# Hymba layer: later-half queries alone in the recurrence levels, and another order of heads and projection steps

## The chip, the cores and the metric

The kernel runs on one core of a Trainium2 chip. The core has five engines with a queue of their own: TensorE (PE in the profile, with its weight loads as PEld), VectorE (DVE), ScalarE (ACT), GpSimd (POOL) and SyncE (SP), which here only issues DMAs. They wait for each other through semaphores. The metric is the device time of one execution in microseconds, the median of several runs.

## The reference

One decoder layer on 1024 tokens, behind 16 meta tokens (T = 1040 positions), with width 1024: a half-step feed-forward, one input projection, two groups of heads in parallel, an output projection, and a second half-step feed-forward. Of the two groups, four HGRN2 recurrence heads (key and value width 128) concern us, and the output projection that follows. In one head, with f the forget gate, k, q, v from the projection, and blocks of 128 tokens:

```python
bcum = jnp.cumsum(lf, axis=-2)                    # lf = log f, inside a block
o_inter = jnp.einsum('bhtd,bhdv->bhtv', qk * jnp.exp(bcum), S)
decay = jnp.exp(jnp.where(causal, diff, -jnp.inf))        # diff = bcum_t - bcum_s
attn = jnp.einsum('bhtd,bhsd,bhtsd->bhts', qk, kk, decay)
o_intra = jnp.einsum('bhts,bhsv->bhtv', attn, vk)
S_new = (jnp.exp(b_last[:, :, 0, :])[..., None] * S
         + jnp.einsum('bhsd,bhsv->bhdv', kk * jnp.exp(b_last - bcum), vk))
```

The output o = o_inter + o_intra is normed per head, multiplied by a gate, and joined with the other group's output; then h = h + o @ W_out. Everything is float32.

## The kernel before, in words

The kernel goes through its stages one after the other: first feed-forward, input projection beside the other group's heads, the recurrence heads beside half of the output projection, the rest of that projection, second feed-forward. The change lies in the fourth of these stages, and only there does the order of instructions differ.

**One recurrence head** (`hgrn_attend`, from L799) keeps keys `KB`, queries `QA`, gates `F` and values `vT` in SBUF, with the key dimension on the partitions and time along the free dimension. Loads L805 go through SP's queue; buffers have three copies, so head 3 uses those that head 0 leaves. The steps, each ended by a `yield` with an estimated time of work and a delay in ns:

1. loads; 2. the values are turned by PE (`flip`, L1036) and copied to `vr`.
3. The diagonal of `attn`: products of keys and queries for the 8 blocks of 128 tokens, masked with the identity (L833). Then POOL multiplies the queries with their gates (L839).
4. Seven levels n = 1, 2, ..., 64 (`LEVELS`). In level n a block is cut into pieces of 2n tokens. Queries in the later half of a piece see keys in its earlier half; the decay between them is already in `QA` and `KB`. The products of level n (L827) are taken for all pairs of a block, and a mask picks those of the level (L836, a copy under a byte mask). Afterwards POOL multiplies the later-half queries (L854) and DVE the earlier-half keys (L858) with the products of gates over their half, and DVE halves the table of gate products `Ts` (L864).
5. The keys are turned (`km` L870, `knp` L877), the gate values are loaded into the buffer of `KB` (L880).
6. The states `S`, in the buffer of `F`: PE makes the updates (`up` L891), DVE adds them in a chain of seven (L894).
7. and 8. The outputs, four blocks at a time (L904, L907); ACT squares them (L912), ACT and DVE make the norm.
9. and 10. The outputs are turned back (L923), multiplied with the gate (L925) and split into a rounded part and a rest (L930 on ACT, L931 on POOL).

In step 4, before, four blocks share a PSUM tile of 128 x 512, so a level takes two tiles and two masked copies. The pool `pz2` has two such banks; turns and states share two banks of `ptr2`, outputs two of `po2`.

**The order.** PE's order is written out by `weave`: it is the order in which the steps are called. `weave` keeps a clock of estimated work, a list of heads with the time at which each is due, and a filling stream: the steps of the output projection with the other group's half of o (`mix_out`, k0 = 4, 64 steps of three products each, 16 additions L1210 with a residual from DRAM). Heads 0, 1 and 2 are three lanes; head 3 follows head 0 in its lane. If no head is due, the filling stream goes on, as long as its share of its total is not over the heads' share of theirs (`work`); otherwise the head that is due first takes a step. The orders on the other engines are found by the framework's scheduler from the same program.

Of the kernel before, what the change touches and what calls it, by code (L numbers as in the profile page):

```python
# [39 lines left out]
class Block:  # L40
# [756 lines left out]
    def hgrn_attend(self, h, pool, src, oH):  # L797
        nc = self.nc

        def tile_of(name, n):  # L800
            return pool.tile([P, n], F32, tag=name, name=name, bufs=3)
# [2 lines left out]
        for t, x in ((vT, "v"), (KB, "k"), (QA, "q"), (F, "f")):  # L804
            nc.sync.dma_start(t, src[x][h])  # L805
        vr = tile_of("vr", SEQ).rearrange("p (c d) -> p c d", d=P)
        attn = [tile_of(f"attn{i}", 512).rearrange("p (c t) -> p c t", t=P) for i in range(2)]
        Ts = tile_of("Ts", T // 2 + T // 4 + T // 8 + T // 16 + SEQ // 32 + SEQ // 64 + 16)
        vm, kms = (
            pool.tile([META, P], F32, tag=x, name=x, bufs=3) for x in ("vm", "kms")  # L810
# [8 lines left out]
            nc.scalar.copy(vr[:, 4 * q : 4 * q + 4, :], ps)  # L819
        yield 960, 500  # L820

        def level(i):
            for half in range(2):
                ps = self.pz.tile([P, 4, P], F32, tag="z", name="lvl")
                for j in range(4):
                    c = 4 * half + j
                    nc.tensor.matmul(  # L827
                        ps[:, j, :], KB[:, META + c * P : META + (c + 1) * P],
                        QA[:, c * P : (c + 1) * P], start=True, stop=True,
                    )  # L830
                if i is None:
                    m = self.ident.unsqueeze(1).broadcast_to([P, 4, P])
                    nc.vector.tensor_mul(attn[half], ps, m)  # L833
                else:
                    m = self.masks[:, i, :].unsqueeze(1).broadcast_to([P, 4, P])
                    nc.vector.copy_predicated(attn[half], m, ps)  # L836

        level(None)
        nc.gpsimd.tensor_mul(QA, QA, F[:, META:])  # L839
        yield 1740, 3200  # L840
        tn = F
        at = 0
        for i, n in enumerate(LEVELS):
            level(i)
            if n <= 8:
                kb = KB.rearrange("p (b h r) -> p b h r", h=2, r=n)
                tk = tn[:, : T // n].rearrange("p (b h) -> p b h", h=2)
            else:
                kb = KB[:, META:].rearrange("p (b h r) -> p b h r", h=2, r=n)
                tk = tn[:, 1 : 1 + SEQ // n].rearrange("p (b h) -> p b h", h=2)  # L850
            nb = kb.shape[1]
            qa = QA.rearrange("p (b h r) -> p b h r", h=2, r=n)
            nq = qa.shape[1]
            nc.gpsimd.tensor_mul(  # L854
                qa[:, :, 1, :], qa[:, :, 1, :],
                tk[:, nb - nq :, 0:1].broadcast_to([P, nq, n]),
            )
            nc.vector.tensor_mul(  # L858
                kb[:, :, 0, :], kb[:, :, 0, :], tk[:, :, 1:2].broadcast_to([P, nb, n])
            )  # L860
            o = 0 if n <= 8 else 1
            nt = Ts[:, at : at + nb + o]
            at += nb + o
            nc.vector.tensor_mul(nt[:, o : o + nb], tk[:, :, 0], tk[:, :, 1])  # L864
            tn = nt
            yield 1740, 2600
# [390 lines left out]
    def weave(self, fill, streams=(), total=0.0, work=0.0):  # L1257

        clock = spent = done = 0.0
        live = [[0.0, s] for s in streams]
        ended = []
        join = None
        filling = True
        while live or filling:
            live.sort(key=lambda e: e[0])  # L1270
            if join is not None and any(e is join for e in ended):
                join = None
            ready = bool(live) and live[0][0] <= clock
            even = not work or spent * work <= (done + 6000) * total
            if not ready and filling and join is None and (even or not live):
                step = next(fill, None)
                if step is None:
                    filling = False
                elif isinstance(step, tuple):
                    if step[0] == "start":  # L1280
                        live.append([clock, step[1]])
                    elif not any(e is step[1] for e in ended):
                        join = step[1]
                else:
                    clock += step
                    spent += step
                continue
            entry = live[0]
            clock = max(clock, entry[0])
            step = next(entry[1], None)  # L1290
            if step is None:
                live.remove(entry)
                ended.append(entry[1])
            else:
                clock += step[0]
                done += step[0]
                entry[0] = clock + step[1]

    def run(self):
# [20 lines left out]
        with ExitStack() as c0:  # L1320
# [217 lines left out]
            with tc.manual_schedule(engines={nc.tensor.engine}), ExitStack() as cx:  # L1538
                with ExitStack() as c1:
                    mix = self.pool("mix2", ctx=c1)  # L1540
                    self.weights("wo", 2, 2, c1)
                    ho = self.pool("ho", ctx=c1)
                    oH.extend([ho.tile([P, 4, 512], F32R, name=f"oH{x}{i}") for i in range(2)]
                              for x in range(2))
                    self.pproj = self.pool("pproj2", 2, PSUM, c1)

                    def from_dram(half):
                        got = []
                        for i in range(2):
                            t = self.pool_o.tile([P, 4, 512], F32R, name=f"oT{half}{i}")  # L1550
                            nc.sync.dma_start(
                                t.bitcast(F32),
                                oD[:, :, i, 512 * half : 512 * half + 512]
                                .rearrange("k p t -> p k t"),
                            )
                            got.append(t)
                        return got

                    def first_half_of_o():
                        o = [from_dram(half) for half in range(2)]  # L1560
                        yield 5000.0
                        plan = [(m, half) for m in range(KT) for half in range(2)]
                        for t, f in self.mix_out(4, plan, o, {}, hD, hT, mix):
                            f()
                            yield t

                    with ExitStack() as c2:
                        c2.push(hg_ctx)
                        self.pool_o = self.pool("oT", ctx=c2, side="right")
                        self.pz = self.pool("pz2", 2, PSUM, c2)  # L1570
                        self.ptr = self.pool("ptr2", 2, PSUM, c2)
                        self.po = self.pool("po2", 2, PSUM, c2)
                        lanes = [chain(heads[0], heads[3]), heads[1], heads[2]]
                        self.weave(first_half_of_o(), lanes, 64 * 650.0 + 5000.0, 4 * 20000.0)
                    xa = self.pool("xs_a", ctx=cx, side="right")
                    operands(xa, ("B11", "B21"))
                    ev0 = self.pool("ev0", ctx=cx, side="right")
                    pre = ExitStack()
                    px = self.pool("pre", ctx=pre, side="right")
                    pps = self.pool("pps", 2, PSUM, c1)  # L1580
                    sums = [px.tile([P, n], F32, tag="nacc", name="nacc", bufs=2) for _ in "ab"]

                    def summed(half, c):

                        plan = [(m, half) for m in range(KT)]
                        steps = self.mix_out(0, plan, oH, ws, hD, hT, mix)
                        for i, (_, f) in enumerate(steps):
                            f()
                            if i % 4 == 3 and i > 3:
                                self.square(sums[half], hT, i // 4 - 1, c, n, px)  # L1590
                            yield i
                        self.square(sums[half], hT, KT - 1, c, n, px)

                    ws = {}
                    self.weights("wo2", 2, KT, c1)
                    drain(summed(0, cA))
                    blocks = iter(())
                    for i in summed(1, cB):
                        if i == 4:
                            r = self.inv_rms_rows(sums[0], n, px, pps)  # L1600
                        if i == 7:
                            r = self.spread_rows(r, n, px, pps)
                            blocks = self.blocks_a(hT, self.g2, cA, n, r, ops)
                        if i % 2:
                            next(blocks, None)
                    drain(blocks)
# [67 lines left out]
```

## Time and profile before

| | us |
|---|---|
| median of 3 runs | 2162.69 (2160.17 to 2167.77) |
| the profiled execution, its own time | 2161.26 |
| its span, first to last instruction | 2159.5 |
| from the first diagonal product of heads 0 to 2 to the end of their last level | 1273.86 to 1335.69 |
| from there to head 3's diagonal | 1335.69 to 1377.18 |
| head 3's diagonal and levels beside the output projection | 1377.18 to 1414.40 |
| rest of head 3, to the end of that half of the projection | 1414.40 to 1440 |

Times inside the trace are us from the start of the span. A row of a timeline has the start, the duration of the merged group, the engine, the line, the operation, its tiles and the number of merged instructions; in brackets stands the idle time before it and what ended it. A float32 product appears as two records on PE. The granted TensorE clock was 0.991 of full speed over the execution.

### The profile page before, as it was taken

To read this page: it belongs to the slowest core of one execution; us is meant where nothing else is said; L and a number is where in the kernel's file an instruction comes from. 1 tells how busy PE (TensorE), PEld (TensorE's weight loads), DVE (VectorE), ACT (ScalarE), POOL (GpSimd) and SP (SyncE) were. 2 spreads that over 40 slices of the span, in tenths; PEclk is the share of its full clock that TensorE was granted. 3 is DMA by queue.
4 is the path that set the end of the run, shared out by engine and by line. 5 is a ranking of instruction groups with operands and counts; after the bars stand their busy time and mean duration, and the time that the engine had idled before them with its cause. 6 is when DMAs were issued, how large, how long until landed. Compare 5 with 4: busy or idle time off the path is not lost.

```text
span 2159.5 us, 32075 instructions
## 1 busy us (share of the span) xinstructions
PE 2053.0 (95%) x11520; PEld 1838.6 (85%) x11520; DVE 1384.6 (64%) x2058; ACT 892.5 (41%) x1809; POOL 701.7 (32%) x764
## 2 busy tenths in 40 slices
PE   6899999999999999999999987899899999999998
PEld 6899999999999989987787876777678888878887
DVE  5775554554589842256766668658867667677674
ACT  8543333333465534455656520324323323334443
POOL 2265545452000313233332333312455445440000
PEclk9999999999999999999999999999999999999999
DMA  6543333334867636433443161233533333248363
GB/s 173 164 153 116 123 104 102 100 120 147 258 207 219 211 102 187 148 109 97 130 130 112 50 250 40 88 108 114 179 103 107 99 107 113 89 166 297 102 202 135
DMA packets 263440, 300.19 MB, mean 139 GB/s; under 512 B 24657, under 2 KB 189521, under 8 KB 262769
## 3 DMA queue, kind: packets, MB, share of 16 engines
q1 hardware_dynamic: 244784, 244.88, 37.0%
q0 software_dynamic: 17456, 53.26, 6.8%
q8 instruction: 91, 1.49, 0.3%
q14 instruction: 69, 0.56, 0.1%
q10 hardware_dynamic: 1040, 0.00, 0.0%
HBM read 215.96 MB, written 82.11 MB: 138 GB/s over the span
## 4 chain that ended last, share of the span: by engine, by line
PE 41%; DVE 6%; issue 2%; ACT 2%; POOL 1%; DMA 1%; SPq 0%; DVEq 0%; POOLq 0%; ACTq 0%
PE o L586 9%; PE qb L319 8%; PE qc L319 5%; PE qa L319 5%; PE lvl L827 2%; PE wo L163 1%; PE wo L164 1%; PE wo L162 1%; PE proj L162 1%; DVE keep L1179 1%; PE proj L163 1%; PE proj L164 1%; PE flip L1036 1%; DMA vT<-hg_v 1%; POOL sig L1182 1%
## 5 line engine op out<-in xcount | busy, mean ns | idle before, releaser
L319 PE MATMUL qb<-T,wh 128*128 128x344 f32 (+1 forms) x1056 | 312.7, 359 | 14.2 <-DVE u L361 10.3
L278 DVE TENSOR_TENSOR wl<-s,wh 128x512 fp32r<-128x512 f32 x176 | 202.9, 1153 | 117.7 <-ACT wh L276 114.9
L319 PEld LDWEIGHTS qb<-T,wh 128*128 128x128 f32 x1056 | 193.7, 190 | 40.5 <-ACT wh L276 8.9
L586 PE MATMUL o<-th,wh 128*128 128x344 f32 (+1 forms) x616 | 218.5, 356 | 4.0 <-DVE hT L596 4.0
L586 PE MATMUL o<-tl,wh 128*128 128x344 f32 (+1 forms) x616 | 218.5, 356 | 3.4 <-DVE tl L517 3.4
L586 PE MATMUL o<-th,wl 128*128 128x344 f32 (+1 forms) x616 | 218.3, 356 | 0.9 <-DVE wl L517 0.7
L319 PE MATMUL qa<-B,wh 128*128 128x344 f32 (+1 forms) x704 | 210.2, 363 | 0.0
L162 PE MATMUL proj<-xh,wh 128*128 128x344 f32 (+2 forms) x576 | 204.9, 356 | 0.9 <-ACT xh L1412 0.9
L276 ACT CAST wh<-s 128x512 fp32r<-128x512 f32 x176 | 109.4, 621 | 226.4 <-PE qb L319 157.3
L164 PE MATMUL proj<-xl,wh 128*128 128x344 f32 (+2 forms) x576 | 199.5, 346 | 0.4 <-POOL xl L1413 0.4
L163 PE MATMUL proj<-xh,wl 128*128 128x344 f32 (+2 forms) x576 | 199.8, 347 | 0.0
L278 DVE TENSOR_TENSOR wl<-raw,wh 128x512 fp32r<-128x512 f32 x172 | 152.2, 888 | 71.8 <-ACT wh L276 67.9
L319 PE MATMUL qb<-T,wl 128*128 128x344 f32 (+1 forms) x528 | 188.7, 357 | 0.0
L276 ACT CAST wh<-raw 128x512 fp32r<-128x512 f32 x172 | 106.0, 620 | 198.4 <-PE qc L319 97.8
L319 PE MATMUL qd<-X,wh 128*128 128x352 f32 x704 | 181.8, 326 | 0.0
L515 ACT CAST th<-act 128x512 fp32r<-128x512 f32 (+2 forms) x176 | 95.1, 542 | 181.0 <-PE o L586 128.2
L291 POOL TENSOR_TENSOR s<-raw 128x512 f32<-128x512 f32 x88 | 120.4, 1368 | 106.5 <-DVE wl L278 73.2
L517 DVE TENSOR_TENSOR tl<-act,th 128x512 fp32r<-128x512 f32 (+2 forms) x176 | 109.9, 628 | 65.6 <-ACT th L515 65.5
L319 PEld LDWEIGHTS qa<-B,wh 128*128 128x128 f32 x704 | 129.5, 190 | 16.0
L1182 POOL TENSOR_TENSOR sig<-sig,keep 128x144 f32<-128x144 f32 (+3 forms) x64 | 80.2, 1253 | 177.9 <-DVE keep L1179 114.0
L586 PEld LDWEIGHTS o<-tl,wh 128*128 128x128 f32 x616 | 116.3, 189 | 17.3 <-DVE tl L517 5.3
L319 PE MATMUL qa<-B,wl 128*128 128x344 f32 (+1 forms) x352 | 127.0, 361 | 4.0 <-DVE wl L278 4.0
(328 smaller groups left out, 4971.4 us busy)
## 6 DMA issues: line engine op xcount, KB each, us to landing
raw<-in_ffn_w_in_dram SPq DMA_DIRECT2D x208, 256.0 KB, 3.0
raw<-in_ffn_w_out_dram SPq DMA_DIRECT2D x176, 256.0 KB, 4.0
raw<-in_w_in_dram SPq DMA_DIRECT2D x28, 512.0 KB, 3.8
ks<-kD SPq DMA_DIRECT2D x32, 260.0 KB, 5.3
ak<-in_ffn_w_out_dram SPq DMA_DIRECT2D x22, 256.0 KB, 4.9
hT<-xD SPq DMA_DIRECT2D x8, 520.0 KB, 9.3
xD<-xts POOLq DMA_DIRECT2D x16, 256.0 KB, 3.0
vD<-vhl SPq DMA_DIRECT2D x8, 512.0 KB, 4.7
```

Source lines behind the costliest of these rows:

```text
L162: nc.tensor.matmul(ps, wh[:, s], xs, start=k == 0, stop=False)
L163: nc.tensor.matmul(ps, wl[:, s], xs, start=False, stop=False)
L164: nc.tensor.matmul(ps, wh[:, s], xl[:, k, c0 : c0 + n], start=False, stop=k == nk - 1)
L276: nc.scalar.copy(hi, src)
L278: nc.vector.tensor_sub(lo, src, hi.bitcast(F32))
L291: op(t, x, y)
L319: nc.tensor.matmul(ps, a[:, k, :], b[:, k0 + k, :], start=start and k == 0 and i == 0, stop=k == 3 and i == 2, skip_group_check=True,)
L515: nc.scalar.copy(hi, src)
L517: nc.vector.tensor_sub(lo, src, hi.bitcast(F32))
L586: nc.tensor.matmul(banks[bank][m], y[:, m * P : (m + 1) * P], z, start=start and q == 0 and e == 0, stop=q == nq - 1 and e == 2, skip_grou ...
L827: nc.tensor.matmul(ps[:, j, :], KB[:, META + c * P : META + (c + 1) * P], QA[:, c * P : (c + 1) * P], start=True, stop=True,)
L1182: nc.gpsimd.tensor_mul(sig, sig, keep[:, 1 : nk + 1])
```

## The change

Four things change.

- The diagonal keeps its two tiles, in a function of its own. A level computes products for later-half queries alone: 64 of the 128 columns of a block, so all 8 blocks fit one tile of 128 x 512 (one bank). One masked copy then goes over all eight blocks, and touches only the later-half columns of `attn`. For that the two `attn` tiles of a head become one of 1024 columns.
- `weave`, where it has a budget (`work`), takes among the heads that are due the one in the lowest lane, where it took the one that was due first.
- The budget for the four heads goes from 4 x 20000 to 4 x 21900.
- What follows from these for the order on PE: heads 0 and 1 start their diagonal before head 2 turns its values, and head 2 runs about a level behind them. Two steps of the projection come behind the key turns of heads 0 and 1, two behind the last level of head 2, one before and one after the second output halves of heads 0 and 1, four behind their last turns. Where the two orders differ they have the same 16 steps. From head 3's second level on the order is the same as before.

```diff
@@ -804,7 +804,8 @@
         vr = tile_of("vr", SEQ).rearrange("p (c d) -> p c d", d=P)
-        attn = [tile_of(f"attn{i}", 512).rearrange("p (c t) -> p c t", t=P) for i in range(2)]
+        at8 = tile_of("attn", SEQ).rearrange("p (c t) -> p c t", t=P)
+        attn = [at8[:, 4 * i : 4 * i + 4, :] for i in range(2)]
@@ -819,7 +820,7 @@
-        def level(i):
+        def diagonal():
             for half in range(2):
                 ps = self.pz.tile([P, 4, P], F32, tag="z", name="lvl")
                 for j in range(4):
@@ -828,20 +829,33 @@
                         ps[:, j, :], KB[:, META + c * P : META + (c + 1) * P],
                         QA[:, c * P : (c + 1) * P], start=True, stop=True,
                     )
-                if i is None:
-                    m = self.ident.unsqueeze(1).broadcast_to([P, 4, P])
-                    nc.vector.tensor_mul(attn[half], ps, m)
-                else:
-                    m = self.masks[:, i, :].unsqueeze(1).broadcast_to([P, 4, P])
-                    nc.vector.copy_predicated(attn[half], m, ps)
-
-        level(None)
+                m = self.ident.unsqueeze(1).broadcast_to([P, 4, P])
+                nc.vector.tensor_mul(attn[half], ps, m)
+
+        def later(x, n):
+
+            return x.rearrange("p (b h r) -> p b h r", h=2, r=n)[:, :, 1, :]
+
+        def level(i, n):
+            ps = self.pz.tile([P, 8, P // 2], F32, tag="z", name="lvl")
+            for c in range(8):
+                nc.tensor.matmul(
+                    ps[:, c, :].rearrange("p (b r) -> p b r", r=n),
+                    KB[:, META + c * P : META + (c + 1) * P],
+                    later(QA[:, c * P : (c + 1) * P], n), start=True, stop=True,
+                )
+            nb = P // (2 * n)
+            m = later(self.masks[:, i, :], n).unsqueeze(1).broadcast_to([P, 8, nb, n])
+            out = at8.rearrange("p c (b h r) -> p c b h r", h=2, r=n)[:, :, :, 1, :]
+            nc.vector.copy_predicated(out, m, ps.rearrange("p c (b r) -> p c b r", r=n))
+
+        diagonal()
         nc.gpsimd.tensor_mul(QA, QA, F[:, META:])
         yield 1740, 3200
...
         for i, n in enumerate(LEVELS):
-            level(i)
+            level(i, n)
@@ -1261,13 +1275,17 @@
         clock = spent = done = 0.0
-        live = [[0.0, s] for s in streams]
+        live = [[0.0, s, i] for i, s in enumerate(streams)]
...
         while live or filling:
-            live.sort(key=lambda e: e[0])
+            if work:
+                live.sort(key=lambda e: (max(e[0] - clock, 0.0), e[2]))
+            else:
+                live.sort(key=lambda e: e[0])
@@ -1278,7 +1296,7 @@
                     if step[0] == "start":
-                        live.append([clock, step[1]])
+                        live.append([clock, step[1], 0])
@@ -1571,7 +1589,7 @@
                         lanes = [chain(heads[0], heads[3]), heads[1], heads[2]]
-                        self.weave(first_half_of_o(), lanes, 64 * 650.0 + 5000.0, 4 * 20000.0)
+                        self.weave(first_half_of_o(), lanes, 64 * 650.0 + 5000.0, 4 * 21900.0)
```

## The prediction

> **What bounds the kernel now.** I read the page first, then the busy time by stretch around the changed stage, then the tile of the level products, then that stage engine by engine in order of time.
>
> ```profile
> span 2159.5 us, 32075 instructions
> PE 2053.0 (95%) x11520; PEld 1838.6 (85%) x11520; DVE 1384.6 (64%) x2058; ACT 892.5 (41%) x1809; POOL 701.7 (32%) x764
> ```
>
> On average PE is the bound with 95%, so a change that relieves DVE would be worth nothing. The average hides the stage that is changed:
>
> ```profile
> core 0: us, PE busy (x) PEld busy (x) DVE busy (x) ACT busy (x) POOL busy (x), PEclk, DMA share, GB/s
> 1269.14:1273.86 4.72, 3.87 (x28) 2.84 (x27) 3.44 (x11) 3.03 (x6) 0.00 (x0) 1.00 1.02 390
> 1273.86:1335.69 61.83, 50.76 (x386) 46.37 (x385) 58.82 (x76) 2.08 (x4) 31.11 (x23) 0.97 0.30 103
> 1335.69:1377.18 41.49, 31.41 (x227) 26.68 (x225) 23.41 (x52) 19.57 (x69) 8.06 (x7) 1.00 0.30 97
> 1377.18:1414.40 37.22, 37.22 (x228) 32.82 (x227) 28.80 (x40) 2.57 (x5) 11.84 (x9) 1.00 0.30 86
> 1414.40:1440.00 25.60, 25.03 (x139) 20.69 (x137) 11.69 (x24) 7.97 (x26) 1.42 (x2) 1.00 0.32 93
> ```
>
> Each row has the length of a stretch, then the busy time of PE, PEld, DVE, ACT and POOL. From 1273.86 to 1335.69 heads 0 to 2 go through the diagonal and the seven levels: DVE is busy 58.82 of 61.83 us, PE 50.76. Here DVE is the bound. From 1335.69 to 1377.18 the heads build their states and outputs, and PE is idle 10.1 of 41.49 us. From 1377.18 on head 3 runs alone between steps of the output projection, and PE is full: nothing can be gained there except by less PE work. So at most 11.1 + 10.1 + about 1.4 us = 23 us of PE idle time lie in reach, 1% of the span.
>
> ```profile
> L827 PEld LDWEIGHTS lvl<-QA,KB x512: 186/192/338, 1273.8 to 1411.4; 128*128 128x128 f32 x171
> L827 PE MATMUL lvl<-QA,KB x512: 270/275/553, 1273.9 to 1411.5; 128*128 128x128 f32 x171
> L836 DVE COPY_PREDICATED attn<-masks,lvl x56: 710/722/746, 1283.9 to 1411.8; 128x512 f32<-128x512 uint8 x56
> L833 DVE TENSOR_TENSOR attn<-lvl,ident x8: 673/688/692, 1275.0 to 1379.9; 128x512 f32<-128x512 f32 x8
> ```
>
> 256 products appear as 512 records, two to an fp32 product; 56 masked copies are 4 heads x 7 levels x 2 halves. One beat late in the three-head stretch, DVE, then POOL, then PE:
>
> ```profile
> 1315.57 0.74 DVE L836 COPY_PREDICATED attn<-masks,lvl 128x512 f32<-128x512 uint8 x1 [0.16 <-PE lvl L827]
> 1316.19 1.13 DVE L858 TENSOR_TENSOR KB<-KB,Ts 128x520 f32<-128x520 f32 x1
> 1317.25 1.32 DVE L836 COPY_PREDICATED attn<-masks,lvl 128x512 f32<-128x512 uint8 x2
> 1318.47 0.88 DVE L858 TENSOR_TENSOR KB<-KB,Ts 128x512 f32<-128x512 f32 x1
> 1319.27 0.73 DVE L836 COPY_PREDICATED attn<-masks,lvl 128x512 f32<-128x512 uint8 x1
> ```
>
> ```profile
> 1315.67 1.10 POOL L854 TENSOR_TENSOR QA<-QA,Ts 128x512 f32<-128x512 f32 x1 [1.61 <-issue]
> 1317.72 1.08 POOL L854 TENSOR_TENSOR QA<-QA,Ts 128x512 f32<-128x512 f32 x1 [0.95 <-PE lvl L827]
> ```
>
> ```profile
> 1313.51 4.07 PE L827 MATMUL lvl<-QA,KB 128*128 128x128 f32 x32 [0.70 <-DVE attn L836]
> 1318.10 4.07 PE L827 MATMUL lvl<-QA,KB 128*128 128x128 f32 x32 [0.53 <-DVE attn L836]
> ```
>
> PE does two heads (32 records) in 1318.10 - 1313.51 = 4.59 us, 2.29 us a head-level, and each time waits for a masked copy to free one of two PSUM banks. Copies that follow each other start 0.61 us apart (1317.25 + 1.32 - 0.72 = 1317.85). The KB update takes longest when POOL works: both KB rows end 0.55 us after a POOL product ends (1316.77 to 1317.32; 1318.80 to 1319.35).
>
> **The change part by part.**
>
> *Masked copies.* A level has one copy over 512 elements in place of two: 28 fewer on DVE, 21 of them in the three-head stretch, where DVE is the bound. Each frees a slot of 0.61 us: 21 x 0.61 = 12.8 us. The new copy writes 512 elements in runs of n with steps of 2n, and reads the mask so. No row shows a stepped masked copy; the nearest are the KB updates, which at n = 1 work on every second element:
>
> ```profile
> L858 DVE TENSOR_TENSOR KB<-KB,Ts x17: 680/1070/1427, 1294.0 to 1334.5; 128x520 f32<-128x520 f32 x9, 128x512 f32<-128x512 f32 x8
> L858 DVE TENSOR_TENSOR KB<-KB,F x3: 680/1519/1549, 1285.4 to 1292.0; 128x520 f32<-128x520 f32 x3
> L854 POOL TENSOR_TENSOR QA<-QA,Ts x18: 1048/1088/1300, 1293.5 to 1336.0; 128x512 f32<-128x512 f32 x18
> L854 POOL TENSOR_TENSOR QA<-QA,F x3: 1498/1508/1512, 1284.9 to 1289.9; 128x512 f32<-128x512 f32 x3
> ```
>
> Their least time is 680 ns for the stepped 520 (the F row, n = 1) as for the later ones with long runs, so a step costs DVE nothing there. POOL does mind: 1508 at n = 1 against 1048 at n = 64. I take 0.72 for the new copy. The ends are 0.72 and, if it slowed as POOL does, 0.72 x 1508/1048 = 1.04, which takes 21 x 0.32 = 6.7 us back if all levels had it; most have longer runs, so about 3.
>
> *Level products.* 224 products go from 128 moving columns to 64; each still loads the same 128 columns of KB. Whether that saves PE time is told by products with fewer moving columns:
>
> ```profile
> 1489.45 1.05 PE L175 MATMUL nps<-ones_d,nacc 128*128 128x1 f32 x8 [2.23 <-DVE nacc L210]
> 1405.29 1.95 PE L827 MATMUL lvl<-QA,KB 128*128 128x128 f32 x16
> 1409.85 1.95 PE L827 MATMUL lvl<-QA,KB 128*128 128x128 f32 x16
> ```
>
> With one moving column eight records take (1.05 - 0.25)/7 = 0.114 us each; with 128 moving columns sixteen take (1.95 - 0.27)/15 = 0.112 (0.25 and 0.27 for the last record's own time; its PEld stream is as long). One column costs as much as 128: loading the weights sets the pace. So 64 columns cost 0.112 too, and I book 0. The ends: 0, and half the stream, 16 x 0.056 = 0.9 us a head-level. The moving operand is also read in steps; at twice the time a column it would still lie under the load.
>
> The Trainium skill, "TensorE: Matmul & The Clock Gate", section "LDWEIGHTS (loading the stationary operand)", puts a load at columns/1.2 ns, 107 ns for 128, whatever moves; the trace agrees (112). The table under "Back-to-back issue gap" of the same page lets a matmul fall with its moving columns, to about 60 cycles for 64 or fewer; taken alone it speaks for a gain on PE, which the one-column rows contradict.
>
> *Three-head stretch, sum.* DVE: 61.83 - 12.8 = 49.0 us. The floor is PE: 3 heads x 8 x 16 records x 0.112 = 43.0 us. So DVE still sets it, with little over; -12.8 stands, and -18.8 is its end.
>
> *One bank a level.* Two levels instead of one are in flight in two banks, so the bank wait is for the copy of the head before last. Booked at nothing of its own: DVE's queue behind it sets the time.
>
> *The order of heads.* Heads 0 and 1 now start their diagonal before head 2 turns its values, and head 2 stays a level behind. On POOL its gate product moves behind two level-1 products:
>
> ```profile
> 1275.89 7.44 POOL L839 TENSOR_TENSOR QA<-QA,F 128x1024 f32<-128x1024 f32 x3 [21.28 <-PE lvl L827]
> ```
>
> 2.5 us each, so head 2 waits 2 x 1.5 = 3.0 us longer; PE has the second level of heads 0 and 1 in front (2 x 1.8 us), so it costs 0; uncovered it costs 3.0. On DVE head 2's small Ts products now stand between level copies, and what waits behind them is the next copy and its bank; there are as many as before, so 0.
>
> *States and outputs.* PE's order from here until head 3's second level has the same products and the same 16 output-projection steps; only their places differ. Before, the output products wait for squares:
>
> ```profile
> 1358.80 0.46 PE L904 MATMUL op<-F,QA 128*128 128x128 f32 x2 [2.51 <-ACT sq L912]
> 1363.84 0.46 PE L904 MATMUL op<-F,QA 128*128 128x128 f32 x2 [1.23 <-ACT sq L912]
> 1350.69 2.71 DVE L894 SCALAR_TENSOR_TENSOR F<-F,Ts,up 128x128 f32<-128x128 f32 x7 [0.61 <-PE up L891]
> ```
>
> Now head 2's turns and a projection step stand between the two halves of heads 0 and 1, so 2.51 + 1.23 = 3.7 us go. What is late next: the transposes of head 0's output come right behind head 2's state products and need their two banks, which DVE's chain of seven (2.71 us) frees; PE stands there about 2.7 us. Net -1.0, ends -6 and +5.
>
> *DMAs.* SP's queue gets a weight load and a residual load among the gate loads, and head 3's four loads stay behind all three gate loads:
>
> ```profile
> L805 SPq DMA_DIRECT2D F<-hg_f x4: 319/350/461, 1256.9 to 1363.2; - x4
> DMA to landing us min/median/max: 3.2/7.8/10.4
> ```
>
> Head 3's F goes into head 0's buffer, free after head 0's second output half. DVE's next use of it, the first Ts product of head 3, stands ahead of head 2's state updates and head 0's gain. By my walk it is reached some 5 us after the issue, so the 3.2 to 5 us that a lone pair needs is covered, the 10.4 of twelve loads together is not: 0, ends 0 and +5.
>
> *The tail.* From head 3's second level on the order is the same, four projection steps between levels, and PE stays full (levels start 1409.85 - 1405.29 = 4.56 us apart). 0. The budget's new constant moves only steps ahead of it.
>
> **Sum.** -12.8 + 0 - 1.0 + 0 = -13.8 us on the profiled execution: 2159.5 + 1.8 around it = 2161.3, so 2147.5. The median of the three runs, 2162.7, lies 1.4 above that execution; I say 2148.
>
> **Rivals.**
>
> *PE gains too.* If 64 columns take half the stream, each of head 3's seven levels shrinks by 0.9: 6.3 us in the full stretch, and about 1 where DVE sets the time: 2140. Against it stand the one-column rows.
>
> *POOL takes the gain back.* With one copy, KB starts 0.61 after the copy. If DVE has once fallen behind by a little, KB of one head meets POOL's product for the next, starts after it, and ends 0.55 behind its end; then copy, bank, products follow in a ring of two banks: 0.61 + 1.7 (copy late) + 0.14 + 1.94 = 4.4 us for two head-levels, 2.2 each in place of 2.29. Then 15 head-levels gain 0.09 and the first six 0.61: 1.4 + 3.7 + 1.0 = 6 us, 2155. The rows with KB 0.55 behind POOL speak for it; against it, that PE's pace of 1.8 leaves 0.2 us a head-level, enough to stay in step.
> The Trainium skill, "SBUF — State Buffer", section "Who interferes with whom", says that a DVE instruction with two SBUF inputs and a GpSimd instruction that reads SBUF block each other wholly, the first to issue winning; the KB rows agree for POOL first, and no row shows POOL held by KB.
>
> *Slower: the steps.* A masked copy with steps of 2n and byte masks is in no row. At three times its time, 2.2 us, it loses 2.2 - 1.33 = 0.87 against the two old ones: 21 x 0.87 = 18 us, 2178. It decides from 1.33 us a copy (no gain), and from 1.69 the kernel is measurably slower. The KB rows speak against it.
>
> *The queue stands.* Head 3's F late by 5 us: 2153.
>
> **How the numbers follow.** Forecast 0.50 (2143 to 2153 alone); PE gains 0.13; POOL 0.20, on the line between faster and same; queue 0.07; steps 0.10. A difference under 0.3% (6.5 us) can't be told from none here. Faster: 0.50 + 0.13 + 0.07 + half of 0.20 = 0.80; same 0.11 (the other half and a tenth of the steps); slower 0.09. The range 2137 to 2160 leaves out the steps and the outer halves of the others.
>
> **What would show it.** Right: L836's successor has 28 copies near 0.72; the 64-column records stay 0.11 apart; the three-head stretch is near 49 us with PE above 85% busy; head 3's levels stay 4.56 apart. Wrong: copies above 1 us, KB updates mostly above 1.3 us with head-levels 2.2 apart, a DVE wait of microseconds on head 3's F, or 64-column records at 0.06.

## The result, and the profile after

The changed kernel takes 2181.07 us (median; 2179.71 to 2182.60) beside 2163.99 us for the kernel before: ratio 1.0079, 95% interval 1.0059 to 1.0099. It is slower by 0.8%, where 2148 us and a gain of 0.7% were forecast. The profiled execution of it has a span of 2178.0 us, 18.5 more than before.

The head of the page of the changed kernel, and its row of granted clocks in 40 slices:

```profile
span 2178.0 us, 32021 instructions
...
PE 2078.3 (95%) x11520; PEld 1867.5 (86%) x11520; DVE 1365.1 (63%) x2030; ACT 892.1 (41%) x1809; POOL 701.6 (32%) x764
...
PEclk9999999999999999999999985999999999999999
```

DVE has 28 instructions and 19.5 us of work less, as the change means it to. PE has the same 11520 records and 25.3 us more of busy time. The row of clocks points at the reason: two slices, 54 us each, stand at 8 and 5 tenths; the execution's mean clock is 0.976, before 0.991.

Busy time by stretch for the changed kernel: the three heads from their first diagonal product to the first key turn, then on to head 3's key turn; below it 20 us inside the three heads, and the same 20 us of the kernel before.

```profile
core 0: us, PE busy (x) PEld busy (x) DVE busy (x) ACT busy (x) POOL busy (x), PEclk, DMA share, GB/s
1272.68:1350.66 77.98, 72.69 (x379) 72.24 (x378) 47.82 (x57) 3.15 (x6) 30.15 (x22) 0.60 0.24 87
1350.66:1433.14 82.48, 72.98 (x470) 63.54 (x470) 48.06 (x89) 22.14 (x73) 20.69 (x16) 0.95 0.29 90
...
1300.00:1320.00 20.00, 20.00 (x96) 20.00 (x95) 11.27 (x12) 0.00 (x0) 7.11 (x6) 0.50 0.00 1
```

```profile
1300.00:1320.00 20.00, 16.17 (x127) 14.59 (x125) 19.71 (x26) 0.00 (x0) 8.70 (x8) 1.00 0.06 14
...
1335.69:1414.42 78.73, 68.65 (x455) 59.50 (x452) 52.21 (x92) 22.14 (x73) 19.89 (x15) 1.00 0.30 91
```

The three-head stretch takes 77.98 us in place of 61.83: +16.2. The next one takes 82.48 in place of 78.73: +3.8; its first 8.7 us still run at half clock. The first product starts 1.2 us earlier (1272.68 after 1273.86), and what follows head 3's key turn is 0.2 shorter: together the 18.5 us. In the 20 us the bound has changed hands. Before, DVE was busy 19.71 of 20 us and PE did 127 records at a clock of 1.00. Now PE is busy without a break, does 96 records at 0.50, and DVE is idle 8.7 us.

PE of the changed kernel in order of time, from head 2's turns into the levels:

```profile
1280.24 0.66 PE L1050 MATMUL flip<-ident,vT 128*128 128x128 f32 x4 [3.05 <-DVE vm L817]
1280.73 6.86 PE L842 MATMUL lvl<-QA,KB 128*128 128x64 f32 x32
1287.39 3.72 PE L828 MATMUL lvl<-QA,KB 128*128 128x128 f32 x16
1290.91 3.75 PE L842 MATMUL lvl<-QA,KB 128*128 128x64 f32 x32
1296.90 49.48 PE L842 MATMUL lvl<-QA,KB 128*128 128x64 f32 x235 [2.24 <-DVE attn L850]
```

The last row holds 235 records without a pause: (49.48 - 0.42)/234 = 0.210 us each on average (the first microsecond still at full clock), where 0.112 was forecast; a head-level of 16 takes 3.4 us in place of the 2.29 of before. The 32 records at 1290.91 have 64 columns too and took (3.75 - 0.27)/31 = 0.112. So it isn't the width as such: the same product costs 0.112 or 0.210, by the clock. The trace's clock record has 0.5 from 1280.8 for 10.2 us and from 1297.9 for 61.4 us, 0.6 and 1.0 us after the end of a pause of PE (3.05 and 2.24 us). The first of these stretches outlasts 6.9 us of 64-column products and ends, at 1291.0, within head 2's diagonal, whose products have 128 columns. The second pause ended with a masked copy, for which DVE came late: ahead of it stood a product of head 2's table `Ts` and a split of projection weights.

```profile
1291.76 2.09 DVE L878 TENSOR_TENSOR Ts<-Ts 128x260 f32<-128x260 f32 x1
1293.77 1.78 DVE L149 TENSOR_TENSOR wl<-raw,wh 128x512 fp32r<-128x512 f32 x1
1295.47 1.28 DVE L850 COPY_PREDICATED attn<-masks,lvl 128x512 f32<-128x512 uint8 x1
```

Later in the levels DVE waits for PE each time, and the copies are shorter:

```profile
1327.01 0.70 DVE L850 COPY_PREDICATED attn<-masks,lvl 128x512 f32<-128x512 uint8 x1 [1.68 <-PE lvl L842]
1327.62 1.13 DVE L872 TENSOR_TENSOR KB<-KB,Ts 128x512 f32<-128x512 f32 x1
1330.43 0.71 DVE L850 COPY_PREDICATED attn<-masks,lvl 128x512 f32<-128x512 uint8 x1 [1.68 <-PE lvl L842]
```

Head 3's levels, which alternate with four projection steps, stay at full clock and 4.57 us apart:

```profile
1405.70 1.90 PE L842 MATMUL lvl<-QA,KB 128*128 128x64 f32 x16
...
1410.28 1.89 PE L842 MATMUL lvl<-QA,KB 128*128 128x64 f32 x16
...
1414.85 1.89 PE L842 MATMUL lvl<-QA,KB 128*128 128x64 f32 x16
```

A pause and a lowered clock stand in the trace of before as well, at the same place. Its PE row, and its busy times in the 3.4 us at which its clock record has 0.5:

```profile
1281.87 5.60 PE L827 MATMUL lvl<-QA,KB 128*128 128x128 f32 x32 [2.17 <-DVE attn L833]
```

```profile
1282.80:1286.20 3.40, 3.40 (x17) 3.18 (x17) 3.25 (x6) 0.00 (x0) 1.81 (x2) 0.50 1.05 386
```

There it came back after 3.4 us, over products of 128 columns. That difference is what the experiments are about.

### The profile page after: what moved, and what is told of

Same layout as the page of the kernel before. It is cut to its first block, busy times and chain, and to the rows that moved or that the text cites. A ratio compares the mean times of both kernels' runs of the same rounds, so it can differ in the third digit from the quotient of the medians.

```text
span 2178.0 us, 32021 instructions
## 1 busy us (share of the span) xinstructions
PE 2078.3 (95%) x11520; PEld 1867.5 (86%) x11520; DVE 1365.1 (63%) x2030; ACT 892.1 (41%) x1809; POOL 701.6 (32%) x764
## 4 chain that ended last, share of the span: by engine, by line
PE 44%; DVE 5%; issue 2%; ACT 1%; POOL 1%; DMA 0%; SPq 0%; DVEq 0%; POOLq 0%; ACTq 0%
PE o L586 9%; PE qb L319 8%; PE qa L319 5%; PE qc L319 5%; PE lvl L842 3%; PE proj L162 1%; PE proj L163 1%; PE proj L164 1%; PE wo L162 1%; PE wo L163 1%; PE wo L164 1%; DVE keep L1193 1%; PE flip L1050 1%; PE oacc L1124 1%; POOL sig L1196 1%
## 5 line engine op out<-in xcount | busy, mean ns | idle before, releaser
L319 PE MATMUL qb<-T,wh 128*128 128x344 f32 (+1 forms) x1056 | 312.3, 358 | 14.1 <-DVE u L361 10.2
```

Source lines behind the costliest of these rows:

```text
L319: nc.tensor.matmul(ps, a[:, k, :], b[:, k0 + k, :], start=start and k == 0 and i == 0, stop=k == 3 and i == 2, skip_group_check=True,)
```

## The experiments

Times are medians, ratios are to the kernel before run beside each kernel. Where no interval stands, the kernel was timed once.

### Products alone, order alone

`e1_width` has the new levels with the old choice of heads and the old budget; `e2_order` has the old levels with the new choice and budget.

```diff
# e1_width, against the changed kernel
-            if work:
-                live.sort(key=lambda e: (max(e[0] - clock, 0.0), e[2]))
-            else:
-                live.sort(key=lambda e: e[0])
+            live.sort(key=lambda e: e[0])
...
-  ..., 64 * 650.0 + 5000.0, 4 * 21900.0)
+  ..., 64 * 650.0 + 5000.0, 4 * 20000.0)
```

> The new levels (64 moving columns, one copy) in the old order of heads, with the old budget. Gate theory (products with 64 columns under a 128-column weight load use the array too little, so the granted clock drops to 0.5 and stays there as long as such products follow each other): clock 0.5 for most of the three-head stretch, records 0.21 us apart, 2175 to 2185 us. Order theory (PE's idle gap of 3 us, which the new order brings ahead of the levels, is needed for the drop): clock stays at 1, about 2150. Step theory (reading the moving operand in steps costs double at any clock): records 0.21 apart at a clock of 1, about 2178.

> The new order and budget with the old levels (128 columns, two banks, two copies). Gate theory: the clock drops for a window or two after the gap of 3 us and comes back, since products of 128 columns use the array fully; 2155 to 2167 us. Order theory: the order itself costs the time, 2175 to 2182. Step theory: as the gate theory.

Measured: products alone 2186.94 us, ratio 1.0108 (1.0084 to 1.0132); order alone 2164.02 us, ratio 1.0002 (0.9987 to 1.0017). Busy times of `e1_width` inside the three heads:

```profile
1300.00:1340.00 40.00, 40.00 (x190) 40.00 (x189) 21.09 (x27) 0.00 (x0) 12.65 (x13) 0.50 0.00 1
```

The loss comes with the products; the order alone shows none. `e1_width` came out above the 2175 to 2185 us of the gate theory. With the old order the clock stands at half for 88.7 us from 1281.5 on, right behind a pause of 2.17 us that the kernel before has too, so the gap of 3 us isn't needed for it, and the new order even shortens it. In `e2_order` the clock is at half three times for 3.4 us only (from 1280.5, 1294.1 and 1345.3 on). Its stretch between the key turns of the first head and of head 3, which has the last of these in it, takes 79.90 us against 78.73:

```profile
1335.20:1415.10 79.90, 71.73 (x471) 62.62 (x469) 51.07 (x95) 21.87 (x73) 21.29 (x16) 0.98 0.29 90
```

### Later-half copies over products of all columns

`e3_all_columns` keeps the new order and the later-half copies, but its products have 128 columns, in two banks with a copy of 256 elements each.

```diff
+            for half in range(2):
+                ps = self.pz.tile([P, 4, P], F32, tag="z", name="lvl")
...
+                        ps[:, j, :], KB[:, META + c * P : META + (c + 1) * P],
+                        QA[:, c * P : (c + 1) * P], start=True, stop=True,
...
+                nc.vector.copy_predicated(out, m, new)
```

> The new kernel, but the products keep all 128 moving columns and two banks, and two copies of 256 elements take the later halves alone. Gate theory: clock near 1; DVE has two copies of about 0.45 in place of two of 0.72, so 21 x 0.5 us less in the three-head stretch, with PE's floor near: 2148 to 2156. Order theory: 2165 to 2175. Step theory: as the gate theory, since the moving operand is read without steps (a slow copy would show in the copies' rows).

Measured: 2159.22 us, ratio 0.9971 (0.9957 to 0.9985). In the changed stage the clock is at half for single stretches of 3.4 us only. DVE's work falls (the copies take 0.42 to 0.45 us, 0.71 to 0.81 at n = 1 and 2), yet the gain is 4.7 us, less than the 8 and more that were expected. PE, POOL and DVE of this kernel:

```profile
1315.83 3.91 PE L846 MATMUL lvl<-QA,KB 128*128 128x128 f32 x32 [0.37 <-DVE attn L854]
1320.14 3.87 PE L846 MATMUL lvl<-QA,KB 128*128 128x128 f32 x32 [0.40 <-DVE attn L854]
```

```profile
1322.31 1.06 POOL L872 TENSOR_TENSOR QA<-QA,Ts 128x512 f32<-128x512 f32 x1 [1.37 <-PE lvl L846]
```

```profile
1322.20 0.45 DVE L854 COPY_PREDICATED attn<-masks,lvl 128x256 f32<-128x256 uint8 x1 [0.36 <-PE lvl L846]
1322.54 1.38 DVE L876 TENSOR_TENSOR KB<-KB,Ts 128x512 f32<-128x512 f32 x1
```

A pair of head-levels takes 4.31 us, 2.15 each: the KB update meets POOL's product, ends 0.55 us after it (1323.92 after 1323.37), and the bank comes late. That is the beat of the rival in which POOL takes the gain back (2.2 forecast there), in this kernel and not in the changed one. That this beat is what keeps the gain small is argued, not shown: no run takes POOL's products away.

### Is it the step of the moving operand?

`e4_no_step` takes 64 consecutive columns in place of stepped ones.

```diff
-                    ps[:, c, :].rearrange("p (b r) -> p b r", r=n),
-                    KB[:, META + c * P : META + (c + 1) * P],
-                    later(QA[:, c * P : (c + 1) * P], n), start=True, stop=True,
+                    ps[:, c, :], KB[:, META + c * P : META + (c + 1) * P],
+                    QA[:, c * P + P // 2 : (c + 1) * P], start=True, stop=True,
```

> The new kernel, but each level's product reads 64 columns that follow each other (the second half of the block at every level) in place of the stepped ones; so the off-diagonal weights are wrong at all levels but the last. Gate theory: nothing changes, clock 0.5, records 0.21 apart, 2176 to 2183. Step theory: records 0.11 apart at a clock of 1, about 2148. Order theory: as the gate theory.

Measured: 2183.24 us. Inside the three heads:

```profile
1300.00:1340.00 40.00, 40.00 (x189) 40.00 (x189) 21.47 (x26) 0.00 (x0) 13.02 (x12) 0.50 0.00 1
```

The same 0.50, over the same stretches as in the changed kernel (10.2 and 61.4 us). So the step isn't what holds the clock down.

### How many columns does the clock ask for?

`e8_columns_96` and `e10_columns_80` have the order of the changed kernel, two banks, and 96 or 80 consecutive columns a product.

```diff
+                        ps[:, j, :96], KB[:, META + c * P : META + (c + 1) * P],
+                        QA[:, c * P + 32 : (c + 1) * P], start=True, stop=True,
```

> As the run with all columns, but each level's products move only 96 columns (and the copies read 64 of them in a row, so the off-diagonal weights are wrong). Gate theory, with the drop decided by how long the array is used: 96 columns use it for three quarters of the weight load's time, which would hold the clock at 1 if the threshold lies between a half and three quarters: 2155 to 2163. If any shortfall lets it drop: clock 0.5, records 0.21 apart, 2180 or more.

> As the run with 96 moving columns, with 80 (columns 48 to 127 of each block; all weights off the diagonal but those of the last level are wrong, so the output is not the reference's). If the clock asks for only a little more than half of the load's columns, it stays at 1 here too, and the time is that of 96 columns, 2160 to 2163 us. If it asks for more than five eighths, the clock is at 0.5 through the three heads, records 0.21 us apart, and the time is 2180 to 2187 us. A clock that goes up and down would give a time between.

Measured: 2160.70 us with 96 columns, 2180.50 with 80. Busy times of the first, then of the second:

```profile
1296.00:1330.00 34.00, 29.51 (x241) 27.75 (x240) 31.82 (x49) 0.00 (x0) 17.48 (x15) 1.00 0.03 9
```

```profile
1292.00:1350.00 58.00, 58.00 (x274) 58.00 (x274) 37.45 (x52) 0.00 (x0) 20.04 (x17) 0.50 0.02 5
```

Under a load of 128 columns, 96 moving columns get the clock back (after 6.8 and 3.4 us at half) and 80 don't, in one run of each, although PE is idle in the first (29.51 of 34 us busy) and never in the second. That PE is busy is not what brings the clock back.

### Dense products among the 64-column ones

`e5_warm` puts four products of 128 columns, whose result is overwritten, ahead of each level of the changed kernel; `e9_warm_early` does so at n = 1, 2 and 4 alone, `e11_warm_first` at n = 1 alone.

```diff
             ps = self.pz.tile([P, 8, P // 2], F32, tag="z", name="lvl")
+            for c in range(0, 8 if i < 3 else 0, 2):     # e5_warm: range(0, 8, 2); e11_warm_first: i < 1
+                nc.tensor.matmul(
+                    ps[:, c : c + 2, :].rearrange("p c r -> p (c r)"), self.ident, self.ones_d,
+                    start=True, stop=True,
+                )
```

> The new kernel with four extra products (128 columns of ones, 8 records, 0.9 us at full clock) ahead of each level's 64-column products, which then overwrite them. Gate theory: with a third of the time at full use the clock stays at 1; the 64-column records go back to 0.11 us apart, a head-level takes about 2.7 us, and although PE does 28 x 0.9 = 25 us more work, the time falls below the new kernel's, to 2160 to 2175. Any theory in which 64-column products are slow of themselves: 2181 + 25 = about 2206.

> The changed kernel with four extra 128-column products ahead of the levels n = 1, 2 and 4 alone; from n = 8 on the three heads have 64-column products only, entered at full clock and without a wait of microseconds before them. Theory A, 64-column products by themselves let the clock fall: some microseconds after the last extra product (near 1310 to 1315 us of the trace) the clock goes to 0.5 and stays there to the key turns, records 0.21 us apart; some 12 head-levels at 3.41 in place of 2.68 us, about 2177 to 2182 us in all. Theory B, it was the idle time of 2.2 to 3.1 us ahead of them that made it fall, and 64-column products are only too light to bring it back: the clock stays at 1 from n = 8 on, records 0.11 us apart, the three-head stretch is shorter than with all the extra products by up to 12 x 0.4 us, about 2160 to 2169 us.

> The changed kernel with the four extra 128-column products ahead of level n = 1 alone, so that PE works through most of the wait for POOL's gate product and the two waits that follow; from n = 2 on 64-column products only. If the clock on entering the run of 64-column products decides, and nothing later, it stays at 1 to the key turns: the run with extra products ahead of n = 1, 2 and 4 took 2156.5 us in a single look, and up to six blocks of 0.94 us in the three-head stretch fall away, so 2151 to 2157 us, faster than before by 0.3 to 0.6%. If the extra products at n = 2 and 4 were needed, because waits of some microseconds remain there, the clock falls near 1295 us and stays at half: 2172 to 2181 us.

Measured: `e5_warm` 2173.94 us, ratio 1.0040 (1.0024 to 1.0056): 7 us under the changed kernel, though PE has 28 blocks of 0.94 us more to do. `e9_warm_early` 2156.47 us, beside 2167.30 before, under the range that either theory gave. `e11_warm_first` 2155.82 us, ratio 0.9951 (0.9933 to 0.9968). PE of `e9_warm_early` in its last stretch of levels, then PE, busy times and DVE of `e11_warm_first`:

```profile
1306.64 17.98 PE L847 MATMUL lvl<-QA,KB 128*128 128x64 f32 x160
```

```profile
1279.34 1.12 PE L1055 MATMUL flip<-ident,vT 128*128 128x128 f32 x4 [3.06 <-DVE vm L817]
1280.25 1.91 PE L842 MATMUL lvl<-ones_d,ident 128*128 128x128 f32 x8
1281.96 2.29 PE L847 MATMUL lvl<-QA,KB 128*128 128x64 f32 x16
...
1294.97 28.70 PE L847 MATMUL lvl<-QA,KB 128*128 128x64 f32 x256
```

```profile
1271.77:1294.97 23.20, 18.95 (x147) 18.12 (x146) 18.48 (x27) 3.15 (x6) 12.94 (x7) 0.93 0.79 288
1294.97:1323.50 28.53, 28.53 (x258) 28.53 (x257) 27.44 (x33) 0.00 (x0) 17.82 (x16) 1.00 0.01 2
1323.50:1364.00 40.50, 34.39 (x208) 29.41 (x207) 23.34 (x53) 14.35 (x48) 7.21 (x6) 0.87 0.31 105
```

```profile
1311.20 0.73 DVE L855 COPY_PREDICATED attn<-masks,lvl 128x512 f32<-128x512 uint8 x1
1311.82 1.11 DVE L877 TENSOR_TENSOR KB<-KB,Ts 128x512 f32<-128x512 f32 x1
1312.98 0.71 DVE L855 COPY_PREDICATED attn<-masks,lvl 128x512 f32<-128x512 uint8 x1
```

Here my explanation changed. Up to `e5_warm` I held that 64-column products by themselves let the clock fall. They don't: 256 records in a row, 28.5 us, run at 1.00 and at (28.70 - 0.27)/255 = 0.111 us each. In `e11_warm_first` the clock falls after the same pause as in the changed kernel (at 1279.4, after 3.06 us), comes back after 3.4 us that hold head 2's turns, the extra products and the first 64-column ones, and stays up to the key turns. So it takes two things: a pause lowers the clock, and products of 64 columns, once they run at half, don't bring it back. A pause costs 3.4 us at half clock before the change; in the changed kernel the two cost 10.2 and 61.4 us. That 64-column products hold a full clock rests on the 18.0 us of `e9_warm_early` and the 28.5 us of `e11_warm_first`; no run takes the pauses away and leaves all else as it was.

### Projection steps among the levels

`e6_fill` has the products of `e3_all_columns` and an order of steps written out by hand in place of `weave`'s: 21 projection steps beside the three heads, three instead of four between head 3's levels. `e7_fill_64` has this order with the changed kernel's products, `e12_fill_64_warm` the same with the extra products at n = 1 and 2.

```diff
+PLAN = "0 1 2 L 0 1 2 0 1 2 0 1 F 2 0 1 F 2 ..."     # 0 to 3: a head's step, F: a projection step, L: its loads
+    def planned(self, fill, heads, plan):
+        for x in plan.split():
+            if x in "FL":
+                next(fill)
+            else:
+                next(heads[int(x)])
...
-                        self.weave(first_half_of_o(), lanes, 64 * 650.0 + 5000.0, 4 * 21900.0)
+                        self.planned(first_half_of_o(), heads, PLAN)
```

> Products with all columns, later-half copies, and an order written out that puts 21 of the 64 projection steps beside the three heads' levels, keys, states and outputs, and three in place of four between head 3's levels. Gate theory and the count of PE's idle time (23 us in the stage before): clock near 1, PE idle 8 to 12 us in the stage, 2146 to 2156. If DVE stays the bound in the levels: 2158 to 2164.

> The same order with the new 64-column products and one copy a level. Gate theory: one projection step (0.7 us at full use) to three head-levels of 64 columns is little; if the clock still drops for part of the stretch, 2160 to 2180; if it holds, 2144 to 2154. Any theory in which 64-column products are slow of themselves: 2170 to 2180.

> 64-column products with the written-out order that puts 21 projection steps beside the three heads (2182.7 us without extra products, clock at half for 88.7 us from the wait before level 1), now with the four extra 128-column products ahead of n = 1 and n = 2. If the clock on entry decides: it stays at 1, the three-head stretch has 5.6 us more PE work than with 128-column products in the same order (2148.5 us) and less DVE work, and that order had 6 us of idle PE to take it: 2143 to 2151 us. If the wait for the projection's first weights, 2.1 us at 1298 us, makes it fall again, the rest of the stretch runs at half: 2165 to 2180 us.

Measured: `e6_fill` 2148.48 us, ratio 0.9926 (0.9909 to 0.9942); `e7_fill_64` 2182.67 us, ratio 1.0088 (1.0069 to 1.0107); `e12_fill_64_warm` 2151.93 us, ratio 0.9933 (0.9917 to 0.9950). Busy times of the three in this order, the first and the last over the three heads, the second inside them:

```profile
1272.78:1331.08 58.30, 52.18 (x405) 48.93 (x403) 53.11 (x77) 2.07 (x4) 31.64 (x23) 0.97 0.32 113
```

```profile
1300.00:1340.00 40.00, 39.87 (x176) 38.81 (x177) 18.54 (x26) 0.00 (x0) 10.85 (x10) 0.50 0.05 14
```

```profile
1270.00:1331.00 61.00, 58.15 (x464) 56.47 (x464) 49.26 (x64) 3.78 (x7) 31.16 (x23) 0.94 0.35 125
```

`e7_fill_64` lies above the 2160 to 2180 us that were expected: one projection step (three products of 512 columns) after every three head-levels did not bring the clock back, which stands at half for 88.7 us from 1281.5 on. With the extra products at the start the same order gains 31 us. `e6_fill` and `e12_fill_64_warm` both beat the two kernels of the study; which of them is the better their intervals don't tell.

## Why the prediction was wrong

**The step that failed** is *Level products*, in its words "So 64 columns cost 0.112 too, and I book 0. The ends: 0, and half the stream". The 0.112 holds, but at a granted clock of 1: the rows it was read from, one moving column among them, all stood at 1.00. For most of the three heads the clock was 0.50 and the records came 0.21 us apart, so the term was not 0 but up to 21 head-levels at 3.4 us: +16.2 us in place of -12.8 for the stretch, a miss of 29 of the 32 us in all. The ends allowed for a gain alone, with nothing that excluded a loss. The row that could have raised the question was among the quoted ones: 0.97 for the three-head stretch. It stands for the 3.4 us at half clock after a pause; what ended them, and whether the new products would end them too, wasn't asked.

The Trainium skill, "TensorE: Matmul & The Clock Gate", section "Part 1: The HAM clock gate (the "warmup" mystery)", has a clock that is lowered after an idle window and full again after a busy one, each of about 3.4 us. On the way up the trace agrees for products of 128 and 96 columns (single stretches of 3.4 or 6.8 us at half) and not for 64 and 80: there PE has no idle time for 53 us and more, and the clock stays at 0.50. On the way down pauses shorter than that were enough here (2.17 us before the change).

**Masked copies** (-12.8) came out in sum where the clock holds: in `e11_warm_first` the stretch takes 1323.50 - 1271.77 = 51.7 us, of which the three extra blocks are about 2.8; without them 48.9, against 49.0 forecast. So close a fit is partly luck: 3.4 us of that stretch ran at half clock, and in its last 28.5 us PE was the bound (busy 28.53 of 28.53 us, DVE 27.44), so "So DVE still sets it" is wrong there by a hair. The price of a copy was wrong for two levels of seven: 0.69 to 0.75 us from n = 4 on, but 1.28 to 1.34 at n = 1 and 2, a mean of (2 x 1.31 + 5 x 0.72)/7 = 0.89, between the ends 0.72 and 1.04. What the slower copies cost, no run separates; one of 1.28 us stands at the end of the pause of 2.24 us.

**One bank a level** and **the order of heads** were booked 0. As waits they cost little: order alone is 1.0002, and in `e11_warm_first` PE has no wait in its last 28.5 us of levels. But the wait that the prediction named and booked at 0, for the next copy and its bank behind head 2's `Ts` products, did come: it is the pause of 2.24 us ahead of the 61.4 us at half clock. `e2_order`, with the old banks, has one of 2.94 us at that place, so the single bank isn't shown to be its cause. What the sum had no place for is that a pause of 2 to 3 us, cheap as a wait, lowers the clock for what follows it.

**States and outputs** (-1.0, ends -6 and +5): 79.90 - 78.73 = +1.2 us in `e2_order`, with 3.4 us of it at half clock. In the changed kernel the waits for squares went, as said, and head 0's transposes wait 1.39 and 0.88 us, near the 2.7 booked. Not booked were 0.89 and 0.24 at the outputs, 1.78 at head 2's transposes, and 1.55 at head 3's turns after 1.20 before.

**DMAs** and **the tail** were right: no wait of microseconds on head 3's `F`, levels 4.57 apart against 4.56.

**The rivals.** *POOL takes the gain back* did not happen in the changed kernel, with KB updates of 1.13 us; its beat stands in `e3_all_columns`. *PE gains too* is refuted by 0.111 at full clock. *Slower: the steps* gave 2178 us, near the measured time by accident: its copies of 2.2 us don't exist (1.35 at most). No rival named the clock.

## What to carry to other kernels

Before products are made narrower than their load (here 96 moving columns on a load of 128 brought the clock back, 80 did not), look at the granted clock of the stretch and at what PE waits for ahead of it: a pause that costs 3.4 us at half clock among dense products can cost the whole stretch among narrow ones. Where that is so, a few dense products right behind the pause brought the clock back here, and the narrow ones then ran at it. Real work served as well (head 2's diagonal did so in the changed kernel), but one projection step among three head-levels did not. A duration read from a trace holds at the clock of its row, so the clock belongs beside every PE term of a sum.

## What the runs showed of the hardware

The granted clock doesn't follow from PE being busy. It went to 0.5 after pauses of 1.7 to 3.1 us, or after two shorter ones close together (1.17 and 1.17 us in `e8_columns_96`, 0.92 and 0.45 us behind the key turns in `e2_order`), and came back after 3.4 to 6.8 us over fp32 products of 128 or 96 moving columns on loads of 128; with 80 or 64 columns it stayed at 0.5 for 61 to 89 us, at 0.21 us a record. Run at full clock from the start, 64 columns hold it (28.5 us at 1.00). What is counted, and why a pause of 3.05 us in `e9_warm_early` lowered nothing while 3.06 in `e11_warm_first` did, these runs don't settle.

A copy under a mask that goes over single elements or pairs (n = 1 and 2) takes 1.28 to 1.35 us for 512 elements in the changed kernel and `e11_warm_first`, and 0.71 to 0.81 for 256 in `e3_all_columns`; with runs of four or more 0.69 to 0.75 and 0.42 to 0.45. The KB update over every second element shows nothing of the kind (0.68 us at least, in the kernel before).
